# Rotation tables of an S5 scan as a background task of their own, in a one-core decoder block

## The chip, the core and the metric

The kernel runs on one core of a Trainium2 chip. The time is device microseconds of one launch; lower is better. The kernel's own comparison is a median of three runs.

## The reference

One decoder layer on 256 tokens of width 2048, in float32. Three branches read the same normalised input, are gated, summed and projected, and a squared-ReLU MLP follows.

```python
xn = rms_norm(x, norm_mix_g)
u_s5, u_lru, q, k, v, gate_logits = split(xn @ w_in)          # 2048 -> 5*1024 + 3*2048
g_s5, g_lru, g_attn = split(sigmoid(gate_logits + b_gate))    # three gates, 2048 wide each

# S5: 64 groups of 16 channels and 64 complex states, a diagonal linear recurrence over time
h = linear_scan(lam_bar, b_bar * u_s5)                        # h[t] = lam_bar*h[t-1] + ...
y = gelu(Re(C h) + d * u_s5);  y_s5 = y * sigmoid(y @ w_glu + b_glu)
# RG-LRU: causal convolution, two block-diagonal gates, a real linear recurrence
y_lru = rglru_branch(u_lru)
# stick-breaking attention, 8 heads of 128: exp(log_sigmoid(z) + sums of log_sigmoid(-z)) weights
y_attn = stick_breaking_attention(q, k, v)

h = x + (g_s5*(y_s5 @ w_br_s5) + g_lru*(y_lru @ w_br_lru) + g_attn*(y_attn @ w_br_attn)) @ w_out
out = rms_norm(h + relu(rms_norm(h) @ w_up)**2 @ w_down)
```

## The kernel before, in words

All weights stream through the core once, in **units** of 256 rows by 512 columns (512 KB). The text numbers them from 0 in the order of the list `stream`. For each unit a DMA from SyncE's queue brings `raw`; ScalarE rounds it to `hi` (the CAST of L146); VectorE forms `lo = raw - hi` (L147); TensorE then multiplies with the activations, which are split into hi and lo in the same way: hi·hi, lo·hi and hi·lo, three matmuls of 512 columns. In `chunk_tok` (lines 241 to 243) a unit has 12 such matmuls, in `chunk` (225 to 227) it has 24 of 256 columns. `raw`, `hi` and `lo` have three buffers each, so the CAST of unit i waits until TensorE is done with unit i-3, and the load of unit i until `lo` of unit i-3 is made.

A chunk is all units of 512 output columns. Order of the units: 0 to 31 the inputs of LRU and S5; 32 to 79 four times a gate chunk (8 units) and a branch chunk of the LRU (4 units); 80 to 127 keys, queries and values of two groups of four heads; 128 to 175 four times a gate chunk and a branch chunk of attention; 176 to 191 two gate chunks of S5; 192 to 199 its `w_glu`; then its branch chunks, `w_out` and the MLP. A gate chunk ends with two VectorE operations that add the bias (`gates`, L750) and two Sigmoids on ScalarE (L751); a branch chunk ends with two or four VectorE operations that multiply by the gate and add to `merged` (L760, or L762 and L763).

Everything else runs beside this stream, as generators. `later(gens, rate)` puts a task on the list `side`; after each unit `pump()` gives every task `rate` steps; `finish(task)` takes all the steps that are left. So the source order is: unit, some steps of each task, unit. The tile framework then orders each engine's instructions with a scheduler of its own, within the data dependences, and each engine executes its list strictly in that order; hence a listing of the built program is needed to know what stands behind what.

The S5 scan (`s5_scan`, a task with 1.27 steps per unit) works in 8 blocks b. The complex recurrence is made real by rotating with cosine and sine tables of the phase at each step: `s5_tables(b)` makes the tables `tc` and `ts` of 128x1024 each. Its instructions: a sum of two phase parts on VectorE (L604), rounding to whole turns on ScalarE (an Identity with a large bias, L606) and on VectorE (L607), an Abs on ScalarE (L609) and two Sin on ScalarE (L610, L611). A block needs: four small matmuls `ps_v` and their copies to `s_v` (L652), six multiplications and sums of 128x1024 with the block's own tables (L660 to L670), eight scans (L705), six more such operations (L681 to L692), a matmul `ps_y` and one VectorE operation into `us5` (L700). While a block runs, the tables of the next are made, by `next(more, None)` at three places of the code: the sum of L604 after L670, L606 and L607 after the scans, Abs and both Sin after L683. `s5_split` and `s5_stack` prepare the next block's inputs (VectorE and ScalarE operations into `ux`, twelve DMAs of 64 KB into `stk`).

`gelu` (a Square and a Tanh on ScalarE, two VectorE operations) runs after every second block, as a task. `attention` computes per head a chain of Abs, Exp and Ln on ScalarE (L796 to L798), sums along the keys on TensorE, and one more Exp (L811).

ScalarE holds one set of function tables at a time. Where two functions of different sets follow each other in its list, an ACT_TABLE_LOAD stands between them. Sin is in another set than Sigmoid and Tanh, and Exp and Ln in a third.

Of the kernel before, what the change touches and what calls it, by code (L numbers as in the profile page):

```python
# [46 lines left out]
def hybrid_block(ctx: ExitStack, tc: tile.TileContext, io, out):  # L47
# [61 lines left out]
    raw, hi, anchor = {}, {}, {}  # L109
    st = {"load": 0, "split": 0, "use": 0}  # L110

# [120 lines left out]
    def chunk_tok(name, c, k, xs, hold=0, done=None):  # L232
        ng = k // (P * UK)
# [11 lines left out]
        for g in range(ng - hold):  # L245
            (nm, cc, _), wh, wl = next_unit()
            assert (nm, cc) == (name, c)
            for kk in range(UK):
                for j in range(len(cols)):
                    mm = mms(j, g * UK + kk, wh[:, kk, :], wl[:, kk, :])  # L250
            anchor["pe"] = mm.ins
            pump()
        held = [next_unit() for _ in range(hold)]
# [339 lines left out]
    S5_RATE = 1.27  # L593

    def s5_tables(b):
# [7 lines left out]
        def gen():  # L603
            nc.vector.tensor_tensor(c, fhi[:, q, :].unsqueeze(3).broadcast_to(sh), flo[:, q, :].unsqueeze(2).broadcast_to(sh), ALU.add)  # L604
            yield
            nc.scalar.activation(sf, cf, AF.Identity, bias=magic)  # L606
            nc.vector.scalar_tensor_tensor(sf, sf, -MAGIC, cf, ALU.add, ALU.subtract)  # L607
            yield
            nc.scalar.activation(cf, sf, AF.Abs)  # L609
            nc.scalar.activation(sf, sf, AF.Sin, scale=-TURN)  # L610
            nc.scalar.activation(cf, cf, AF.Sin, scale=-TURN, bias=half_pi)  # L611
            yield
# [18 lines left out]
    def s5_scan():  # L631
# [3 lines left out]
        tabs, more = s5_tables(0)  # L635
        yield from more
        s5_split(0)
        yield
# [4 lines left out]
        tt = nc.vector.tensor_tensor  # L643
        for b in range(WT):
            c, s = tabs
            t3 = pp.tile([P, NT, L], F32, tag="t3", name=f"t3_{b}")
            for t in range(NT):
# [5 lines left out]
                if t % 2:  # L653
                    yield
            more = iter(())
            if b + 1 < WT:
                s5_split(b + 1)
                tabs, more = s5_tables(b + 1)
                yield
            tt(t1, vr, c, ALU.mult)  # L660
# [9 lines left out]
            tt(t3, t3, vr, ALU.subtract)  # L670
            next(more, None)
            yield
            for x_ in (t1, t3):
                for t in range(NT):
# [4 lines left out]
                    yield  # L679
            next(more, None)  # L680
            tt(t2, t1, c, ALU.mult)  # L681
            yield
            tt(vr, t3, s, ALU.mult)  # L683
            next(more, None)
            yield
# [15 lines left out]
            if b % 2:  # L701
                gq.append(later([gelu(b)], 1.0))

    def tt_scan(o, r, i):
        nc.vector.tensor_tensor_scan(o, r, i, 0.0, ALU.mult, ALU.add)  # L705

    def gelu(b):
        y = us5[:, b - 1:b + 1, :]
        g1 = tmp.tile([P, 2, L], F32, tag="gate", name=f"g1_{b}", bufs=3)
        nc.scalar.activation(g1, y, AF.Square)  # L710
        nc.vector.scalar_tensor_tensor(g1, g1, 1.0 / GELU_K, y, ALU.add, ALU.mult)
        yield
        nc.scalar.activation(g1, g1, AF.Tanh, scale=GELU_C * GELU_K)
        nc.vector.scalar_tensor_tensor(y, g1, 1.0, y, ALU.add, ALU.mult)
        yield
# [19 lines left out]
    def gates(idx, c, alloc):  # L735
# [8 lines left out]

        later([bias()], 1.0)
        banks = chunk_tok("w_in", GATE0 + 4 * idx + c, D, xs)
        gts = []
        for j in range(2):
# [36 lines left out]
    def attention(hs, kT, qT, vt):  # L785
# [26 lines left out]

        tc.keep_in_program_order(nc.scalar.preload_act_table_set("natural_log_exp_and_others"))
        yield
        for i in range(7):
            if i >= 3:
                weights(hs[i - 3])
            if i < 4:
                logits(hs[i])
            yield  # L820
        while vt[0] is None:
            yield
# [348 lines left out]
```

## Time and profile before

| | |
|---|---|
| three runs | 1511.58, 1511.49, 1508.52 us; median 1511.49 us |
| the profiled execution | 1512.1 us, its span 1510.3 us |
| busy: TensorE, weight loads, VectorE, ScalarE, GpSimd | 1488.4, 1260.5, 1175.2, 782.3, 35.3 us |
| mean granted clock of TensorE | 0.995 |
| ACT_TABLE_LOADs | 33, of 1283 ns each |

In the profile an instruction is named by its line of the kernel, its engine, and `out<-in` with the tiles' names. A matmul row shows about 0.39 us, but the next one starts 0.227 us later, since matmuls overlap; a wait of TensorE is best read from the starts. The profile names what ended a wait behind an arrow. Times are microseconds from the start of the span.

### The profile page before, as it was taken

What the parts mean: (1) busy time and instruction counts of PE and PEld (TensorE: products, weight loads), DVE (VectorE), ACT (ScalarE), POOL (GpSimd) and SP (SyncE); (2) the same over time, 40 slices, a digit from 0 to 9 for tenths busy, and PEclk for the clock granted to TensorE, in tenths of its full rate; (3) what the DMA queues carried; (4) which work ended last, traced back from release to release, by engine and by line L of the source; (5) the groups of instructions that cost most, each with busy time, mean ns of one, the idle gap of its engine ahead of it and who ended that gap; (6) DMA issues with size and microseconds to landing.
All of it is one profiled execution on the core that took longest, in us unless ns stands there. A gap on an engine that the chain in (4) does not pass through costs nothing.

```text
span 1510.3 us, 19900 instructions
## 1 busy us (share of the span) xinstructions
PE 1488.4 (99%) x7518; PEld 1260.5 (83%) x7518; DVE 1175.2 (78%) x1468; ACT 782.3 (52%) x920; POOL 35.3 (2%) x60
## 2 busy tenths in 40 slices
PE   9999999999999999999999999999999999999997
PEld 9997788989887878988887888888888888888886
DVE  6767998897988989689799796568854787558965
ACT  6767556565765564544455544344433444344443
POOL 1400000000000000000000000000000000000011
PEclk9999999999999999999999999999999999999999
DMA  9546766665555666666855666666666666666664
GB/s 287 157 153 176 228 205 201 187 182 168 175 172 183 208 182 210 189 202 190 276 182 188 197 184 205 194 185 196 198 194 193 193 195 195 195 191 191 192 197 152
DMA packets 89858, 292.41 MB, mean 194 GB/s; under 512 B 12834, under 2 KB 17058, under 8 KB 89634
## 3 DMA queue, kind: packets, MB, share of 16 engines
q1 hardware_dynamic: 89618, 291.07, 62.6%
q8 instruction: 59, 0.97, 0.3%
q14 instruction: 37, 0.30, 0.1%
q10 hardware_dynamic: 144, 0.07, 0.0%
HBM read 282.71 MB, written 2.10 MB: 189 GB/s over the span
## 4 chain that ended last, share of the span: by engine, by line
PE 83%; DVE 9%; issue 3%; ACT 2%; DMA 2%; SPq 0%; DVEq 0%; ACTq 0%
PE mt_w_up L242 6%; PE mt_w_up L241 6%; PE mt_w_up L243 6%; PE mt_w_in L242 5%; PE mt_w_in L243 5%; PE mt_w_in L241 5%; PE mt_w_down L242 4%; PE mt_w_down L241 4%; PE mt_w_down L243 4%; PE mp_w_down L277 4%; PE mp_w_down L278 4%; PE mp_w_down L276 4%; PE mm_w_in L227 4%; PE mm_w_in L225 4%; PE mm_w_in L226 4%; DVE lo L147 3%
## 5 line engine op out<-in xcount | busy, mean ns | idle before, releaser
L146 ACT CAST hi<-raw 128x1024 fp32r<-128x1024 f32 (+1 forms) x521 | 545.2, 1049 | 625.9 <-PE mt_w_up L243 131.4
L147 DVE TENSOR_TENSOR lo<-raw,hi 128x1024 fp32r<-128x1024 f32 (+1 forms) x521 | 637.9, 1225 | 287.7 <-ACT hi L146 284.1
L242 PE MATMUL mt_w_in<-lo,xhi 128*128 128x512 f32 x448 | 176.1, 393 | 3.9 <-DVE lo L147 3.7
L241 PE MATMUL mt_w_in<-hi,xhi 128*128 128x512 f32 x448 | 175.2, 396 | 0.2 <-ACT hi L146 0.2
L243 PE MATMUL mt_w_in<-hi,xlo 128*128 128x512 f32 x448 | 175.2, 391 | 0.0
L241 PE MATMUL mt_w_up<-hi,hhi 128*128 128x512 f32 x448 | 174.3, 389 | 0.0
L242 PE MATMUL mt_w_up<-lo,hhi 128*128 128x512 f32 x448 | 174.3, 389 | 0.0
L243 PE MATMUL mt_w_up<-hi,hlo 128*128 128x512 f32 x448 | 174.3, 389 | 0.0
L227 PE MATMUL mm_w_in<-xhi,lo 128*128 128x256 f32 x512 | 145.4, 286 | 4.5 <-DVE lo L147 4.5
L225 PE MATMUL mm_w_in<-xhi,hi 128*128 128x256 f32 x512 | 146.5, 286 | 0.5 <-ACT hi L146 0.4
L226 PE MATMUL mm_w_in<-xlo,hi 128*128 128x256 f32 x512 | 145.7, 285 | 0.0
L728 DVE STREAM_TRANSPOSE reluT<-relu 32x256 f32<-32x256 f32 x256 | 111.5, 436 | 4.2
L242 PEld LDWEIGHTS mt_w_in<-lo,xhi 128*128 128x128 f32 x448 | 84.6, 189 | 24.0 <-DVE lo L147 7.6
L227 PEld LDWEIGHTS mm_w_in<-xhi,lo 128*128 128x128 f32 x512 | 98.7, 194 | 5.5 <-DVE lo L147 5.5
L242 PE MATMUL mt_w_down<-lo,hd_hi 128*128 128x512 f32 (+1 forms) x272 | 102.5, 377 | 0.0
L241 PE MATMUL mt_w_down<-hi,hd_hi 128*128 128x512 f32 (+1 forms) x272 | 102.4, 377 | 0.0
L243 PE MATMUL mt_w_down<-hi,hd_lo 128*128 128x512 f32 (+1 forms) x272 | 102.4, 376 | 0.0
L225 PEld LDWEIGHTS mm_w_in<-xhi,hi 128*128 128x128 f32 x512 | 99.2, 194 | 1.1 <-ACT hi L146 1.0
L277 PE MATMUL mp_w_down<-lo,hd_hi 128*128 128x512 f32 x256 | 99.8, 390 | 0.1
L278 PE MATMUL mp_w_down<-hi,hd_lo 128*128 128x512 f32 x256 | 99.6, 389 | 0.0
L276 PE MATMUL mp_w_down<-hi,hd_hi 128*128 128x512 f32 x256 | 99.6, 389 | 0.0
L241 PEld LDWEIGHTS mt_w_in<-hi,xhi 128*128 128x128 f32 x448 | 84.5, 189 | 17.8 <-ACT hi L146 0.7
(299 smaller groups left out, 2370.2 us busy)
## 6 DMA issues: line engine op xcount, KB each, us to landing
raw<-in_w_in SPq DMA_DIRECT2D x175, 512.0 KB, 4.3
raw<-in_w_up SPq DMA_DIRECT2D x128, 512.0 KB, 4.2
raw<-in_w_down SPq DMA_DIRECT2D x128, 512.0 KB, 4.2
raw<-in_w_out SPq DMA_DIRECT2D x32, 512.0 KB, 4.2
raw<-in_w_br_lru SPq DMA_DIRECT2D x16, 512.0 KB, 4.6
raw<-in_w_br_attn SPq DMA_DIRECT2D x16, 512.0 KB, 4.1
raw<-in_w_br_s SPq DMA_DIRECT2D x16, 512.0 KB, 4.1
stk<-ux SPq DMA_DIRECT2D x96, 64.0 KB, 4.1
```

Source lines behind the costliest of these rows:

```text
L146: anchor["act"] = nc.scalar.copy(h[:, k, :], r[:, k, :]).ins
L147: anchor["dve"] = nc.vector.tensor_tensor(l_[:, k, :], r[:, k, :], h[:, k, :].bitcast(F32), ALU.subtract).ins
L225: nc.tensor.matmul(o, wh[:, kk, s], xh, start=first and ct % 2 == 0, stop=False, skip_group_check=True)
L226: nc.tensor.matmul(o, wh[:, kk, s], xl, start=False, stop=False, skip_group_check=True)
L227: mm = nc.tensor.matmul(o, wl[:, kk, s], xh, start=False, stop=last and ct % 2 == 1, skip_group_check=True)
L241: nc.tensor.matmul(banks[j], xh[:, s], wh[:, a:b], start=kt == 0, stop=False)
L242: nc.tensor.matmul(banks[j], xh[:, s], wl[:, a:b], start=False, stop=False)
L243: return nc.tensor.matmul(banks[j], xl[:, s], wh[:, a:b], start=False, stop=kt == ng * UK - 1)
L276: nc.tensor.matmul(o, xh[:, s], wh[:, kk, :], start=kt == 0, stop=False)
L277: nc.tensor.matmul(o, xh[:, s], wl[:, kk, :], start=False, stop=False)
L278: mm = nc.tensor.matmul(o, xl[:, s], wh[:, kk, :], start=False, stop=kt == ng * UK - 1)
L728: nc.vector.transpose(d_[32 * a:32 * a + 32, :, :, 32 * b:32 * b + 32], s_[32 * b:32 * b + 32, :, :, 32 * a:32 * a + 32])
```

## The change

The steps of the next block's tables are taken out of `s5_scan` and become a task of their own (`later([chain_of(3, more)], S5_RATE)`): it waits three steps and then runs at 1.27 steps per unit. Two empty steps are put in, and a loop that waits with the Sin while the attention task is in its chains (`st["chain"]`), or while a gate chunk is being multiplied with fewer than three units left (`st["gate"]`, `st["left"]`). GELU's Tanh waits while attention is in its chains. At the head of a block `finish(more)` takes what is left of the tables. The number of instructions is the same on every engine, the 33 table loads included.

```diff
@@ chunk_tok
             anchor["pe"] = mm.ins
+            st["left"] = ng - 1 - g
             pump()
@@ s5_tables
         def gen():
             nc.vector.tensor_tensor(c, fhi[...], flo[...], ALU.add)
             yield
+            yield
             nc.scalar.activation(sf, cf, AF.Identity, bias=magic)
             nc.vector.scalar_tensor_tensor(sf, sf, -MAGIC, cf, ALU.add, ALU.subtract)
             yield
+            yield
             nc.scalar.activation(cf, sf, AF.Abs)
+            yield
+            while st["chain"] or st["gate"] and st["left"] < 3:
+                yield
             nc.scalar.activation(sf, sf, AF.Sin, scale=-TURN)
             nc.scalar.activation(cf, cf, AF.Sin, scale=-TURN, bias=half_pi)
             yield
@@ s5_scan
         tabs, more = s5_tables(0)
         yield from more
+        more = None
...
         for b in range(WT):
+            if more is not None:
+                finish(more)
             c, s = tabs
...
-            more = iter(())
             if b + 1 < WT:
                 s5_split(b + 1)
                 tabs, more = s5_tables(b + 1)
+                more = later([chain_of(3, more)], S5_RATE)
                 yield
...
-            next(more, None)          # at three places of the block
+    def chain_of(n, gen):
+        for _ in range(n):
+            yield
+        yield from gen
@@ gelu
         yield
+        while st["chain"]:
+            yield
         nc.scalar.activation(g1, g1, AF.Tanh, scale=GELU_C * GELU_K)
@@ gates
         later([bias()], 1.0)
+        st["gate"] = True
         banks = chunk_tok("w_in", GATE0 + 4 * idx + c, D, xs)
+        st["gate"] = False
@@ attention
         tc.keep_in_program_order(nc.scalar.preload_act_table_set("natural_log_exp_and_others"))
+        st["chain"] = True
         yield
         for i in range(7):
             ...
+        st["chain"] = False
```

Since the first tables now take more steps too, the whole scan stands two to four units later in the lists than before. Three places show what the scheduler makes of it. From `pump` in `chunk_tok` on, the lines of the changed kernel have numbers that are 1 to 17 higher (the CAST stays L146 and `lo` L147): L616 and L617 are the two Sin, L605 and L609 the VectorE steps of the tables, L766 the Sigmoid, L669 to L679 the first six long operations of a block, L716 its scans, L775 and L777/L778 the ends of the branch chunks.

ScalarE's list at the end of the second gate chunk of attention (units 140 to 147), from the CAST of unit 150 to that of unit 151. Before:

```order
L146 CAST hi_4654<-raw_4623 128x1024
L609 ACTIVATE tc_4380<-ts_4381 128x1024
L610 ACT_TABLE_LOAD
L610 ACTIVATE ts_4381<-ts_4381 128x1024
L751 ACT_TABLE_LOAD
L751 ACTIVATE gate_1_0_4644<-gate_1_0_4644 128x512
L751 ACTIVATE gate_1_1_4647<-gate_1_1_4647 128x512
L611 ACT_TABLE_LOAD
L611 ACTIVATE tc_4380<-tc_4380,half_pi 128x1024
L146 CAST hi_4676<-raw_4652 128x1024
```

After:

```order
L146 CAST hi_4652<-raw_4623 128x1024
L616 ACT_TABLE_LOAD
L616 ACTIVATE ts_4443<-ts_4443 128x1024
L766 ACT_TABLE_LOAD
L766 ACTIVATE gate_1_0_4642<-gate_1_0_4642 128x512
L766 ACTIVATE gate_1_1_4645<-gate_1_1_4645 128x512
L617 ACT_TABLE_LOAD
L617 ACTIVATE tc_4442<-tc_4442,half_pi 128x1024
L146 CAST hi_4673<-raw_4650 128x1024
```

The Abs has left this place; both Sin and the three loads around the Sigmoids have stayed.

VectorE's list in the third gate chunk of the LRU and after it, from `lo` of unit 67 to `lo` of unit 70. Before:

```order
L147 TENSOR_TENSOR lo_2184<-raw_2162,hi_2183 128x1024
L670 TENSOR_TENSOR t_1_2034<-t_1_2034,s_v 128x1024
L604 TENSOR_TENSOR tc_2094<-fhi,flo 128x1024
L705 SCALAR_TENSOR_TENSOR s_t<-rad,s_t 128x256
L147 TENSOR_TENSOR lo_2208<-raw_2181,hi_2207 128x1024
L705 SCALAR_TENSOR_TENSOR s_t<-rad,s_t 128x256
L147 TENSOR_TENSOR lo_2230<-raw_2205,hi_2229 128x1024
L705 SCALAR_TENSOR_TENSOR s_t<-rad,s_t 128x256
L760 TENSOR_TENSOR merged<-mt_w_br_lru_0_64_2160,gate_2_0_2154 128x512
L760 TENSOR_TENSOR merged<-mt_w_br_lru_1_64_2161,gate_2_1_2157 128x512
L147 TENSOR_TENSOR lo_2257<-raw_2227,hi_2256 128x1024
```

After:

```order
L147 TENSOR_TENSOR lo_2181<-raw_2159,hi_2180 128x1024
L673 TENSOR_TENSOR s_t<-s_t 128x1024
L675 TENSOR_TENSOR t_1_2089<-s_v,tc_1695 128x1024
L147 TENSOR_TENSOR lo_2201<-raw_2178,hi_2200 128x1024
L677 TENSOR_TENSOR s_v<-s_v,ts_1696 128x1024
L605 TENSOR_TENSOR tc_2130<-fhi,flo 128x1024
L147 TENSOR_TENSOR lo_2221<-raw_2198,hi_2220 128x1024
L679 TENSOR_TENSOR t_1_2089<-t_1_2089,s_v 128x1024
L609 SCALAR_TENSOR_TENSOR ts_2131<-ts_2131,tc_2130 128x1024
L775 TENSOR_TENSOR merged<-mt_w_br_lru_0_64_2157,gate_2_0_2151 128x512
L775 TENSOR_TENSOR merged<-mt_w_br_lru_1_64_2158,gate_2_1_2154 128x512
L147 TENSOR_TENSOR lo_2247<-raw_2218,hi_2246 128x1024
```

The scan's long operations stand later, so that three of them and both VectorE steps of the next tables (L605, L609) now stand among these four `lo`, in place of three scans (`s_t`).

VectorE's list about the third gate chunk's end of attention, up to `lo` of unit 166. Before, from `lo` of unit 163:

```order
L147 TENSOR_TENSOR lo_4964<-raw_4939,hi_4963 128x1024
L705 SCALAR_TENSOR_TENSOR s_t<-rad,s_t 128x256 x2
L147 TENSOR_TENSOR lo_4990<-raw_4961,hi_4989 128x1024
L705 SCALAR_TENSOR_TENSOR s_t<-rad,s_t 128x256
L762 TENSOR_TENSOR gate_2_0_4931<-mt_w_br_attn_0_160_4937,gate_2_0_4931 128x512
L147 TENSOR_TENSOR lo_5012<-raw_4987,hi_5011 128x1024
L705 SCALAR_TENSOR_TENSOR t_6_4785<-rad,t_6_4785 128x256
L763 TENSOR_TENSOR merged<-merged,gate_2_0_4931 128x512
L762 TENSOR_TENSOR gate_2_1_4934<-mt_w_br_attn_1_160_4938,gate_2_1_4934 128x512
L147 TENSOR_TENSOR lo_5038<-raw_5009,hi_5037 128x1024
```

After, from L605 behind `lo` of unit 163 (L675 stands ahead of that `lo`, L677 behind it):

```order
L605 TENSOR_TENSOR tc_4884<-fhi,flo 128x1024
L679 TENSOR_TENSOR t_6_4821<-t_6_4821,s_v 128x1024
L147 TENSOR_TENSOR lo_4978<-raw_4954,hi_4977 128x1024
L716 SCALAR_TENSOR_TENSOR s_t<-rad,s_t 128x256
L609 SCALAR_TENSOR_TENSOR ts_4885<-ts_4885,tc_4884 128x1024
L147 TENSOR_TENSOR lo_5002<-raw_4975,hi_5001 128x1024
L716 SCALAR_TENSOR_TENSOR s_t<-rad,s_t 128x256
L777 TENSOR_TENSOR gate_2_0_4927<-mt_w_br_attn_0_160_4933,gate_2_0_4927 128x512
L777 TENSOR_TENSOR gate_2_1_4930<-mt_w_br_attn_1_160_4934,gate_2_1_4930 128x512
L778 TENSOR_TENSOR merged<-merged,gate_2_0_4927 128x512
L778 TENSOR_TENSOR merged<-merged,gate_2_1_4930 128x512
L147 TENSOR_TENSOR lo_5031<-raw_4999,hi_5030 128x1024
```

Here too long operations and both table steps have moved in among the `lo`, and the four operations at the end of the branch chunk, spread over three units before, now stand in one piece.

More of the change, by code (lines that the diff above doesn't have):

```diff
@@ L109, in hybrid_block @@
     raw, hi, anchor = {}, {}, {}
-    st = {"load": 0, "split": 0, "use": 0}
+    st = {"load": 0, "split": 0, "use": 0, "gate": False, "left": 0, "chain": False}
     def pieces(i):
@@ L679, in s5_scan @@
                     yield
-            next(more, None)
             tt(t2, t1, c, ALU.mult)
@@ L683, in s5_scan @@
             tt(vr, t3, s, ALU.mult)
-            next(more, None)
             yield
```

## The prediction

> **What bounds the kernel now.** I read the page, then the busy times by stretch, then TensorE's waits in the stretch that the change touches, then the rows about each wait.
>
> ```profile
> span 1510.3 us, 19900 instructions
> PE 1488.4 (99%) x7518; PEld 1260.5 (83%) x7518; DVE 1175.2 (78%) x1468; ACT 782.3 (52%) x920; POOL 35.3 (2%) x60
> ```
>
> TensorE is the bound. The change adds and takes away no matmul, so it can pay only where TensorE waits, and cost only where it makes TensorE wait.
>
> ```profile
> core 0: us, PE busy (x) PEld busy (x) DVE busy (x) ACT busy (x) POOL busy (x), PEclk, DMA share, GB/s
> 113.00:210.00 97.00, 93.43 (x420) 74.63 (x420) 80.69 (x92) 60.25 (x74) 0.00 (x0) 0.98 0.67 199
> 210.00:455.00 245.00, 245.00 (x1531) 217.64 (x1530) 212.89 (x249) 151.22 (x195) 0.00 (x0) 1.00 0.61 184
> 455.00:475.00 20.00, 19.61 (x86) 15.67 (x86) 18.65 (x22) 8.60 (x10) 0.00 (x0) 1.00 0.69 207
> 475.00:495.00 20.00, 17.63 (x75) 13.50 (x77) 15.32 (x17) 13.32 (x14) 0.00 (x0) 0.91 0.44 143
> 495.00:610.00 115.00, 114.93 (x566) 94.17 (x559) 103.94 (x114) 64.70 (x76) 0.00 (x0) 1.00 0.67 204
> ```
>
> The scan's tables are made from 113 to 610 us. TensorE is idle there for 3.57 + 0.39 + 2.37 + 0.07 = 6.4 us, and at the head of two stretches the clock was halved: 0.91 over 20 us means (1 - 0.91) x 20 / 0.5 = 3.6 us at half speed. VectorE is busy for 77% to 93% of these stretches (15.32 of 20, 18.65 of 20 us): it has little left.
>
> ```profile
> PE mt_w_in L242 <- DVE lo L147: 3.7, 5, 1.9
> PE mt_w_br_attn L241 <- ACT hi L146: 2.2, 1, 2.2
> ```
>
> One long wait is ScalarE's (`hi`, behind the sines), five are VectorE's (`lo`). The change is aimed at the first kind. Its new loops wait while the program is written, not on the chip: what they do there is the order alone.
>
> **Step 1, unit 151 (the end of a gate chunk): -2.5 us.** The rows before:
>
> ```profile
> 473.81 1.06 ACT L146 CAST hi<-raw 128x1024 fp32r<-128x1024 f32 x1 [0.49 <-PE mt_w_in L243]
> 474.77 1.05 ACT L609 ACTIVATE tc<-ts 128x1024 f32<-128x1024 f32 x1
> 475.84 1.28 ACT L610 ACT_TABLE_LOAD   x1
> 477.13 1.06 ACT L610 ACTIVATE ts<-ts 128x1024 f32<-128x1024 f32 x1
> 478.20 1.28 ACT L751 ACT_TABLE_LOAD   x1
> 479.50 1.15 ACT L751 ACTIVATE gate<-gate 128x512 f32<-128x512 f32 x2
> 480.65 1.28 ACT L611 ACT_TABLE_LOAD   x1
> 481.95 1.15 ACT L611 ACTIVATE tc<-tc,half_pi 128x1024 f32<-128x1024 f32 x1
> 483.00 2.92 ACT L146 CAST hi<-raw 128x1024 fp32r<-128x1024 f32 x3
> ...
> 481.31 0.39 PE L242 MATMUL mt_w_br_attn<-lo,ya_hi 128*128 128x512 f32 x1
> 481.54 0.39 PE L243 MATMUL mt_w_br_attn<-hi,ya_lo 128*128 128x512 f32 x1
> 484.08 0.73 PE L241 MATMUL mt_w_br_attn<-hi,ya_hi 128*128 128x512 f32 x2 [2.15 <-ACT hi L146]
> 486.06 0.63 PE L242 MATMUL mt_w_br_attn<-lo,ya_hi 128*128 128x512 f32 x1
> 486.48 0.63 PE L243 MATMUL mt_w_br_attn<-hi,ya_lo 128*128 128x512 f32 x1
> ```
>
> The next matmul was due at 481.54 + 0.23 = 481.77 and came at 484.08: 2.31 us. Behind it matmuls start 0.42 us apart (486.06, 486.48), not 0.23: that is the half clock, and 3.6 us of it lose 3.6 x (1 - 0.227/0.42) = 1.65 us. The listing of the changed kernel still has Sin, Sigmoid and Sin with three loads ahead of the CAST of unit 151; only the Abs is gone. So: CAST to 474.87, load to 476.15, Sin to 477.21, load to 478.50, Sigmoids to 479.65, load to 480.93, Sin to 482.08, CAST, which starts 0.1 before that ends, to 483.05. TensorE waits 1.33 us, 0.98 less. A wait that short I expect to leave the clock alone, for the two that halved it lasted 2.06 us (below) and 2.31 us; then 1.65 us go too. Together -2.6, taken as -2.5. Ends: -1.0, if the clock still halves, and -4.0, if the whole wait goes.
>
> The Trainium skill (TensorE: Matmul & The Clock Gate, Part 1, "What's actually happening") lets the clock fall back only after at least one idle window of about 3.4 us. By that rule waits of 2.06 and 2.31 us would not have halved it; the trace disagrees, and I go by the trace. By the rule this step would be worth -1.0 and the sum below would be 1.5 us higher.
>
> **Step 2, units 36 to 57 (the first tables, LRU's end): 0 us.** The rows before:
>
> ```profile
> 125.28 1.20 DVE L607 SCALAR_TENSOR_TENSOR ts<-ts,tc 128x1024 f32<-128x1024 f32 x1
> 127.30 0.69 DVE L573 TENSOR_TENSOR ylru_lo<-lru_xc,ylru_hi 128x512 fp32r<-128x512 f32 x1 [0.81 <-ACT ylru_hi L572]
> 127.90 1.22 DVE L147 TENSOR_TENSOR lo<-raw,hi 128x1024 fp32r<-128x1024 f32 x1
> 129.04 1.26 DVE L570 TENSOR_TENSOR_SCAN lru_tc<-lru_tc,lru_ts 128x256 f32<-128x256 f32 x2
> 130.22 1.20 DVE L147 TENSOR_TENSOR lo<-raw,hi 128x1024 fp32r<-128x1024 f32 x1
> ...
> 126.66 0.61 PE L241 MATMUL mt_w_in<-hi,xhi 128*128 128x512 f32 x2
> 129.18 0.50 PE L242 MATMUL mt_w_in<-lo,xhi 128*128 128x512 f32 x1 [1.91 <-DVE lo L147]
> ```
>
> Long VectorE rows start 1.14 us apart, scans and halves 0.60. TensorE wanted `lo` of unit 36 at 126.66 + 2 x 0.23 = 127.12 and got it at 129.18, 2.06 us late. In the changed list `lo` of unit 36 stands ahead of L609 (L607 of before) and takes its place at 125.28: this wait goes. But before `lo` of unit 37 there stand now a `ylru_lo`, two scans, L609 and the other `ylru_lo`. The first cannot start before 127.30, since it waits for ScalarE; then 127.30 + 0.60 + 1.18 + 1.14 + 0.60 = 130.82, and `lo` ends at 132.04. TensorE, not held up, is through unit 36 at 126.66 + 12 x 0.227 = 129.38 and wants that `lo` at 129.83: a wait of 2.2 us, one unit later, as long as the old one and as likely to halve the clock. Behind it the loads, which follow `lo`, even things out. At unit 55 both Sigmoids, a load and both Sin now stand in one piece between two CASTs, 1.15 + 1.28 + 1.06 + 1.15 = 4.6 us, where two units of TensorE give 2 x 2.72 = 5.4: some tenths of a wait, which the small waits of this stretch that go (of the 3.7 us above) pay. Ends: -3.7, if the 2.06 and its half clock go without a successor; +2.5, if unit 55 waits 1.5 us and the rest stays.
>
> **Step 3, unit 70 (VectorE): +1.0 us.** Rows before: the `lo` of unit 67, the row behind it, the group of the copies of `s_v`, and TensorE's first use of `lo` of unit 70.
>
> ```profile
> 216.46 1.23 DVE L147 TENSOR_TENSOR lo<-raw,hi 128x1024 fp32r<-128x1024 f32 x1
> 217.61 1.22 DVE L670 TENSOR_TENSOR t<-t,s_v 128x1024 f32<-128x1024 f32 x1
> ...
> L652 ACT COPY s_v<-ps_v 128x512 f32<-128x512 f32 x32 | 17.2, 587 | 3.4 <-PE ps_v L650 3.2
> ...
> 228.32 0.39 PE L242 MATMUL mt_w_in<-lo,xhi 128*128 128x512 f32 x1
> ```
>
> By the listing there stand behind this `lo` now six long operations, three `lo` and two halves: 217.61 + 9 x 1.14 + 2 x 0.60 = 229.07. TensorE wants the last of them at 228.32: 0.7 us late, and a unit whose `lo` is late starts with two matmuls on `hi`, which gives 0.2 back. Unit 67's `lo` itself will be later than 217.69, by up to 0.9 us: four copies of `s_v`, 4 x 0.59 us, stand between the CASTs of units 64 and 65 where two stood (1.2 us more, of which some is slack). So 0.5 to 1.5; I take 1.0. The other end is 0, if VectorE gets ahead before.
>
> **Step 4, units 163 to 172: +1.8 us.**
>
> ```profile
> 516.93 1.21 DVE L147 TENSOR_TENSOR lo<-raw,hi 128x1024 fp32r<-128x1024 f32 x1
> ...
> 524.09 0.39 PE L242 MATMUL mt_w_in<-lo,xhi 128*128 128x512 f32 x1
> 529.53 0.39 PE L242 MATMUL mt_w_in<-lo,xhi 128*128 128x512 f32 x1
> ...
> 540.18 0.39 PE L241 MATMUL mt_w_in<-hi,xhi 128*128 128x512 f32 x1
> 540.64 0.50 PE L242 MATMUL mt_w_in<-lo,xhi 128*128 128x512 f32 x1
> ```
>
> The first row is `lo` of unit 162, the matmuls are the first uses of `lo` of units 164, 166 and 170. Behind `lo` of unit 162 there now come L675, `lo`, L677, L605, L679 and `lo` of unit 164: 518.07 + 6 x 1.14 = 524.91, 0.8 us after 524.09. Then a scan, L609, `lo`, a scan, four halves, `lo` of unit 166: 6 x 0.60 + 3 x 1.14 = 7.0, at 531.9; TensorE, 0.9 later than before, wants it at 529.53 + 0.9 + 0.2 = 530.6: another 1.3. With 0.1 lost at each restart, 2.4 us. In return the sines, which stood at units 169 to 171 with their Abs, come where there is room, and the wait at 540.64 (540.18 to 540.64, 0.23 too many) goes with two like it: -0.6. Ends: -0.6 and +3.0.
>
> **Step 5, the rest: +0.5 us.** In units 142 to 147 `lo` of unit 143 becomes punctual and that of unit 146 late, by the same shift; at most the 0.39 us of idle of 455 to 475 can go. The end of the scan stands two units later, and the last values for `w_glu` come as they are wanted. 0 to 1.2 for both. The twelve `stk` DMAs of a block move with the scan on SyncE's queue, past two or three loads of weights each time; they share the loads' bandwidth as before, and I set that at nothing, since DMAs are at 0.44 to 0.69 here. Tables and GELU in the middle (210 to 455 us, no idle) are hidden by TensorE's slow chunks and by attention's extra matmuls, and I count nothing; if that cover is short, the `lo` behind L609 in the key chunk (unit 90) is late next.
>
> **Sum:** -2.5 + 0 + 1.0 + 1.8 + 0.5 = +0.8 us, so a span of 1511.1 and, with the 1.8 us outside it, 1512.9 us. The profiled execution (1512.1) lies 0.6 above the median of the three runs, so **1512.3 us** for a median.
>
> A measurement of this kernel tells 0.2%, 3.0 us, from no change.
>
> **Rivals.**
> *VectorE's piles halve the clock (slower).* The waits of units 55, 70 and 166 are each set at 1 to 1.5 us. At about 2 us within one stretch the clock halves, as in units 36 and 151, at 1.65 us each. Two of them: 0.8 + 3.3 = +4.1, 1515.6 us. For it: VectorE's 93% in 455 to 475 and 90% in 495 to 610, and the packed lists. Against it: before, VectorE's waits at the same density were short but for one.
> *The sines stay where they hurt (slower).* The listing shows three loads in a row at unit 151. If a late `gate` operand takes back the Abs's 1.05 us, the wait stays 2.3 us and the clock halves: +0.8 + 2.5 = +3.3, 1514.8 us.
> *VectorE gets ahead (faster).* While the scan is late it does nothing for VectorE; if that lets `lo` run up to its limit of three buffers, steps 3 and 4 give 0 and -0.6, and the sum is -2.5 + 0 + 0 - 0.6 + 0.5 = -2.6, with a wait less at units 36 and 37 (-2.0) -4.6: 1506.9 us. For it: 210 to 455 has no idle at all. Against it: 9 x 1.14 us is more than the 8.2 us that TensorE needs for three units.
>
> **How the numbers follow.** My forecast, a near tie, 0.53; the piles 0.20, the sines 0.10; VectorE ahead 0.17. The last three lie about or beyond 3.0 us. So faster 0.17, same 0.53, slower 0.30. The range takes the faster rival's end, 1506.5, and the slower one's with a further wait of 1.9 us, 1517.5.
>
> **What would show it.** Right: at unit 151 three loads and a wait of 1.0 to 1.6 us with PEclk 1.00 behind; a wait for `lo` of about 2 us at unit 37 in place of 36; waits for `lo` at units 70, 164 and 166 of 0.5 to 1.5 us. Wrong: no waits there, or half-clock rows behind them.

## Result and profile after

The changed kernel takes 1514.08 us (median of 13 runs, 1512.60 to 1515.15); the kernel before, in runs taken between them, 1511.21 us (13 runs, 1508.52 to 1513.38). The ratio is 1.0019, with a 95% interval of 1.0011 to 1.0027: some 2.9 us slower, where +0.8 was forecast. The profiled execution took 1514.19 us, that of before 1512.1.

The busy times of the five stretches after:

```profile
113.00:210.00 97.00, 93.51 (x416) 75.17 (x417) 78.97 (x90) 59.81 (x72) 0.00 (x0) 0.98 0.67 202
210.00:455.00 245.00, 244.54 (x1531) 217.50 (x1529) 212.96 (x249) 151.40 (x194) 0.00 (x0) 1.00 0.60 184
455.00:475.00 20.00, 19.48 (x86) 15.67 (x85) 19.73 (x23) 9.78 (x10) 0.00 (x0) 1.00 0.66 200
475.00:495.00 20.00, 17.00 (x67) 13.08 (x66) 13.86 (x17) 12.90 (x13) 0.00 (x0) 0.91 0.47 142
495.00:610.00 115.00, 114.07 (x557) 92.05 (x556) 104.97 (x114) 63.40 (x73) 0.00 (x0) 1.00 0.65 202
```

The work is the same and the waits are more: TensorE is idle for 8.4 us from 113 to 610, 6.4 before, and the stretch from 475 to 495 still runs at a mean clock of 0.91. Its waits in that part, by what ended them:

```profile
PE mt_w_in L242 <- DVE lo L147: 5.6, 7, 2.4
PE mt_w_br_attn L241 <- ACT hi L146: 2.4, 1, 2.4
```

The wait that the change was aimed at (`mt_w_br_attn`) has not become shorter, and VectorE's have grown from 3.7 to 5.6 us. Unit by unit, by the start of each unit's first matmul: at unit 34 the execution after is 1.23 us ahead of the one before (a difference from the start of the program, where nothing was changed), at unit 205 it is 1.12 us behind. The 2.35 us between are lost and won so (each row runs from the start of its first unit to the start of the unit behind its last, and both kernels have the same number of matmuls in it):

| units | forecast | measured |
|---|---|---|
| 36 to 62 | 0 | -0.5 |
| 70 | +1.0 | +0.8 |
| 71 to 141 | 0 | -0.6 |
| 142 to 149 | in step 5 | +0.1 |
| 150 to 152 | -2.5 | -0.3 |
| 153 to 157 | nothing named | +1.2 |
| 158 to 176 | +1.8 | +1.1 |
| 190 to 195 | in step 5 | +0.5 |

Unit 151, ScalarE's timeline, then TensorE's:

```profile
470.84 1.05 ACT L146 CAST hi<-raw 128x1024 fp32r<-128x1024 f32 x1 [2.50 <-DMA raw<-in_w_br_attn]
473.63 1.05 ACT L146 CAST hi<-raw 128x1024 fp32r<-128x1024 f32 x1 [1.74 <-DMA raw<-in_w_br_attn]
474.70 1.28 ACT L616 ACT_TABLE_LOAD   x1
476.00 1.06 ACT L616 ACTIVATE ts<-ts 128x1024 f32<-128x1024 f32 x1
477.06 1.28 ACT L766 ACT_TABLE_LOAD   x1
478.36 1.15 ACT L766 ACTIVATE gate<-gate 128x512 f32<-128x512 f32 x2
479.51 1.28 ACT L617 ACT_TABLE_LOAD   x1
480.81 1.15 ACT L617 ACTIVATE tc<-tc,half_pi 128x1024 f32<-128x1024 f32 x1
481.86 2.92 ACT L146 CAST hi<-raw 128x1024 fp32r<-128x1024 f32 x3
...
482.94 1.22 PE L241 MATMUL mt_w_br_attn<-hi,ya_hi 128*128 128x512 f32 x2 [2.40 <-ACT hi L146]
...
484.91 0.63 PE L242 MATMUL mt_w_br_attn<-lo,ya_hi 128*128 128x512 f32 x1
485.34 0.63 PE L243 MATMUL mt_w_br_attn<-hi,ya_lo 128*128 128x512 f32 x1
```

The burst of three loads, two Sin and two Sigmoids is there, without the Abs, 7.2 us between two CASTs. But the CAST ahead of it (unit 150, at 473.63) is now late itself: it had to wait for its weights (`<-DMA raw`). Before, that CAST came as soon as TensorE had freed its buffer (`<-PE`). TensorE waited 2.57 us (2.31 before), and the clock was halved again (0.43 us from 484.91 to 485.34). From CAST to CAST the burst is 1.0 us shorter than before (8.23 us, 9.20 before), but against the start of TensorE's unit 149 its first CAST stands 1.2 us later; so the wait has grown by 0.26 us. That units 150 to 152 together still take 0.3 us less comes from behind the wait, where TensorE lost 0.5 us less; why is open.

VectorE ahead of `lo` of unit 146 (465.81), whose end lets the load of unit 149 go:

```profile
460.69 1.22 DVE L605 TENSOR_TENSOR tc<-fhi,flo 128x1024 f32<-128x1024 f32 x1
461.82 1.22 DVE L147 TENSOR_TENSOR lo<-raw,hi 128x1024 fp32r<-128x1024 f32 x1
462.96 1.22 DVE L679 TENSOR_TENSOR t<-t,s_v 128x1024 f32<-128x1024 f32 x1
464.10 0.69 DVE L716 TENSOR_TENSOR_SCAN s_t<-rad,s_t 128x256 f32<-128x256 f32 x1
464.69 1.21 DVE L609 SCALAR_TENSOR_TENSOR ts<-ts,tc 128x1024 f32<-128x1024 f32 x1
465.81 1.23 DVE L147 TENSOR_TENSOR lo<-raw,hi 128x1024 fp32r<-128x1024 f32 x1
```

No row shows idle time: VectorE is full, and both table steps (L605, L609) stand ahead of that `lo`. The matmuls that waited for a `lo`, in TensorE's timeline, at units 37, 70, 146, 154 and 166:

```profile
131.16 0.79 PE L242 MATMUL mt_w_in<-lo,xhi 128*128 128x512 f32 x1 [2.39 <-DVE lo L147]
...
227.46 0.50 PE L242 MATMUL mt_w_in<-lo,xhi 128*128 128x512 f32 x1 [0.46 <-DVE lo L147]
...
467.09 0.50 PE L242 MATMUL mt_w_in<-lo,xhi 128*128 128x512 f32 x1 [0.52 <-DVE lo L147]
...
494.00 0.50 PE L242 MATMUL mt_w_in<-lo,xhi 128*128 128x512 f32 x1 [0.59 <-DVE lo L147]
...
530.86 0.50 PE L242 MATMUL mt_w_in<-lo,xhi 128*128 128x512 f32 x1 [0.84 <-DVE lo L147]
```

All but the fourth were named in the prediction.

### The profile page after: what moved, and what is told of

Same layout as the page of the kernel before. It is cut to its first block, busy times and chain, and to the rows that moved or that the text cites. A ratio compares the mean times of both kernels' runs of the same rounds, so it can differ in the third digit from the quotient of the medians.

```text
span 1511.9 us, 19898 instructions
## 1 busy us (share of the span) xinstructions
PE 1486.8 (98%) x7518; PEld 1258.4 (83%) x7518; DVE 1176.8 (78%) x1468; ACT 783.0 (52%) x920; POOL 36.0 (2%) x60
## 4 chain that ended last, share of the span: by engine, by line
PE 81%; DVE 10%; ACT 3%; issue 3%; DMA 2%; SPq 0%; DVEq 0%; ACTq 0%
PE mt_w_up L242 6%; PE mt_w_up L241 6%; PE mt_w_up L243 6%; PE mt_w_in L242 5%; PE mt_w_in L243 5%; PE mt_w_in L241 5%; PE mt_w_down L242 4%; PE mt_w_down L241 4%; PE mt_w_down L243 4%; DVE lo L147 4%; PE mp_w_down L278 4%; PE mp_w_down L279 4%; PE mp_w_down L277 4%; PE mm_w_in L227 3%; PE mm_w_in L225 3%; PE mm_w_in L226 3%
## 5 line engine op out<-in xcount | busy, mean ns | idle before, releaser
L146 ACT CAST hi<-raw 128x1024 fp32r<-128x1024 f32 (+1 forms) x521 | 545.8, 1050 | 629.3 <-PE mt_w_up L243 130.6
L147 DVE TENSOR_TENSOR lo<-raw,hi 128x1024 fp32r<-128x1024 f32 (+1 forms) x521 | 638.1, 1226 | 283.3 <-ACT hi L146 279.4
```

Of the source, the lines that this page charges most:

```text
L146: anchor["act"] = nc.scalar.copy(h[:, k, :], r[:, k, :]).ins
L147: anchor["dve"] = nc.vector.tensor_tensor(l_[:, k, :], r[:, k, :], h[:, k, :].bitcast(F32), ALU.subtract).ins
```

## Experiments

Theory A: the change loses at unit 151 what it was to win, because the sines stay between the Sigmoids and the early table steps delay a load; and the same steps make `lo` late at units 70, 146 and 164 to 166. Against it stand B (TensorE would wait at unit 151 anyway, for something else) and C (all `lo` are late since the scan stands two units later, whatever the tables do). Times are medians; the ratio is to the kernel before in the same runs, with its interval.

**1. One table step made short.** Does the late load explain the burst's late start?

```diff
-nc.vector.scalar_tensor_tensor(sf, sf, -MAGIC, cf, ...)
+w_ = 64 if b == 6 else 1024
+nc.vector.scalar_tensor_tensor(sf[:, 0:w_], sf[:, 0:w_], -MAGIC, cf[:, 0:w_], ...)
...                              # both Sin of block 6 get another scale
```

> The changed kernel, but for the tables of block 6 alone the second table step on VectorE (L609) works on 64 of its 1024 columns; the rest of those tables is left unrounded and the two Sin take a smaller scale, so their values mean nothing. The lists of all engines keep their order; only this one instruction, which stands ahead of `lo` of unit 146, is about 1.0 us shorter. Theory A (the Abs's 1.05 us was taken back by loads): `lo` of unit 146 is on time, so the wait of 0.8 us at 467 goes; the load of unit 149, issued behind that `lo`, comes about 1 us earlier, so do the CASTs of units 149 and 150 and the whole burst behind them, and TensorE's wait at unit 151 falls from 2.6 to 1.4 to 1.7 us. If the clock then stays full: 0.8 + 1.0 + 1.65 = 3.4 us less than the changed kernel, 1510.7 us; if it still halves, 1.8 less, 1512.3. Rival B (the operands of the Sigmoids, or the place of the burst itself, set the wait): the wait at unit 151 stays at 2.3 us or more and only the 0.8 goes, 1513.3 us.

1511.87 us, 1.0007 (0.9998 to 1.0016), 2.2 us below the changed kernel. ScalarE's and TensorE's timelines:

```profile
470.74 1.05 ACT L146 CAST hi<-raw 128x1024 fp32r<-128x1024 f32 x1 [1.49 <-DMA raw<-in_w_br_attn]
473.50 1.05 ACT L146 CAST hi<-raw 128x1024 fp32r<-128x1024 f32 x1 [1.70 <-DMA raw<-in_w_br_attn]
...
482.81 0.73 PE L241 MATMUL mt_w_br_attn<-hi,ya_hi 128*128 128x512 f32 x2 [1.96 <-ACT hi L146]
```

TensorE starts unit 146 at 467.01 here and at 465.96 in the changed kernel. Counted from there, the CASTs of units 149 and 150 come 1.15 and 1.18 us earlier, and 0.74 us of the wait at unit 146 are gone. So the one step did hold the loads back, and through them the burst. What the expectation forgot: TensorE, not held up at 146, is itself 0.74 us earlier at unit 151. Its wait there fell only from 2.57 to 2.12 us, and the clock was still halved. Together 1.2 us. By the starts of the units, 0.8 of that comes in units 142 to 149 and 0.55 in units 153 to 157; units 150 to 152 gain nothing (12.53 us, 12.41 in the changed kernel), since the shorter wait was lost again behind it. The median is 0.4 below the time expected with a half clock. The trace has a further 1.3 us in units 36 to 62, which this edit does not touch: no half clock followed the wait at unit 37 this time.

**2. No loop, and 10. half the loop.**

```diff
-while st["chain"] or st["gate"] and st["left"] < 3:     # run 2: no loop at all
-    yield
+while st["chain"]:                                      # run 10: this half alone
+    yield
```

> The changed kernel without the loop that holds the two Sin back. In the lists the Sin of block 6 then stand in one piece between the CASTs of units 148 and 149, and the Sigmoids between those of 149 and 150, with two loads less; at unit 129 they stand singly among attention's last exponentials, with two loads more. Theory A (the loop itself keeps the sines at the end of the gate chunk): the wait at unit 151 and its half clock go, 2.6 + 1.65 = 4.2 us; at unit 129 ScalarE has 4 x 1.28 + 1.06 + 1.15 us and three exponentials and the two copies of v between two CASTs, about 9.5 us where TensorE's next three units give 8.2, which costs 1 to 3.5 us (the latter with a half clock); at unit 53 and 54 nothing changes by more than some tenths. Sum -3.2 to -0.7, 1510.9 to 1513.4 us. Rival B (TensorE waits there for something else, loads of weights): -1 or less at unit 151, and the sum is at or above the changed kernel, 1514 to 1517.

> The changed kernel with the half of the loop alone that holds the Sin back during attention's chains; the half for gate chunks is left out. In the lists the Sin of block 6 stand in one piece behind the CAST of unit 148 and the Sigmoids behind that of 149, as without any loop, while attention's exponentials at unit 129 stay undisturbed; at unit 53 the two Sin stand ahead of the two Sigmoids with two loads, 7.1 us with the CAST's between two CASTs. Theory A (the half for gate chunks costs, the half for chains pays): 4.2 us less at unit 151, 1.5 to 3.5 us more at unit 55 (the latter with a half clock): 1511.4 to 1513.4 us, and 2.3 to 4.4 us less than the run without any loop. Rival B: the wait at unit 151 comes back a unit later; 1514 us or more.

Without the loop 1515.76 us, 1.003 (1.0019 to 1.0042); with the half for chains alone 1509.57 us, 0.9991 (0.9981 to 1.0000), 4.5 below the changed kernel. In both, unit 151 waits for nothing: what B says of that unit falls. But the time without the loop lies in B's range and above A's, because the loss at units 129 to 141 was larger than A had it, and units 53 to 57 lost too, where A saw next to nothing. ScalarE in attention's chain without the loop, and the matmul behind it (unit 130):

```profile
413.03 1.28 ACT L614 ACT_TABLE_LOAD   x1
...
419.68 1.28 ACT L824 ACT_TABLE_LOAD   x1
...
423.64 0.79 PE L241 MATMUL mt_w_in<-hi,xhi 128*128 128x512 f32 x1 [3.49 <-ACT hi L146]
```

Four loads lie between these times, two for each Sin among the Exp. TensorE waits 3.65 us, and two windows of half clock follow (422.22 to 429.04 us): units 129 to 141 take 46.77 us, 40.23 in the changed kernel and in run 10. The half for chains is worth these 6.5 us; the medians of the two runs differ by 6.2. The half for gate chunks costs: it puts off the Sin, which would run in one piece behind the CAST of unit 148, until the gate chunk is over, and so right onto its Sigmoids. Leaving it out has a price of its own at unit 54, a wait of 1.94 us for `hi` and two windows of half clock in the profile of run 10 (1.24 us and one window without the loop); that run still came out 1.8 us below its expected range, in part because the waits at units 164 to 166 shrank too (from 1.35 to 0.54 us).

**3. The sines held out of the branch chunk's start.**

```diff
-while st["chain"] or st["gate"] and st["left"] < 3:
+while st["chain"] or st["gate"] and st["left"] < 3 or st["branch"] and st["left"] > 1:
...                              # st["branch"] is set while a branch chunk is multiplied
```

> The changed kernel with one condition more: the Sin also wait while a branch chunk has more than one unit left. In ScalarE's list the two Sin then stand in one piece, with one load, between the CASTs of units 152 and 153; between 150 and 151 there are only the two Sigmoids. Theory A: the whole wait at unit 151 goes with its half clock, 2.6 + 1.65 = 4.2 us, less a wait of up to 0.8 at unit 153 (load and two Sin, 3.5 us, where TensorE has three units); nothing else moves. 1509.9 to 1510.7 us, which is 0.5 to 1.3 below the kernel before. Rival B (a late load or `lo` shows at the same place): 1.5 or less gained, 1512.6 or more.

1506.68 us, 0.9969 (0.9958 to 0.9981): 7.4 us below the changed kernel, more than A had. ScalarE from the CAST of unit 150, and the stretch:

```profile
471.89 1.05 ACT L146 CAST hi<-raw 128x1024 fp32r<-128x1024 f32 x1 [1.71 <-DMA raw<-in_w_br_attn]
472.85 1.16 ACT L766 ACTIVATE gate<-gate 128x512 f32<-128x512 f32 x2
473.91 1.04 ACT L146 CAST hi<-raw 128x1024 fp32r<-128x1024 f32 x1
...
475.00:495.00 20.00, 20.00 (x102) 16.01 (x101) 19.15 (x21) 11.54 (x12) 0.00 (x0) 1.00 0.63 198
```

The CAST of unit 151 now follows 2.0 us behind that of 150, not 8.2, and the stretch has neither idle time nor half clock. In units 150 to 152 TensorE gains 4.2 us on the changed kernel, as expected: that is what the burst cost.

Another 1.2 us come in units 153 to 157, where the changed kernel waits for `lo` of unit 154. One would take that wait for an echo of the burst, since VectorE stood idle for 6.14 us in front of `lo` of unit 151 and had its list behind it. But run 10 has no burst, and the wait is there all the same. VectorE, and TensorE's matmul behind it, in run 10; then VectorE in run 3:

```profile
489.89 1.28 DVE L777 TENSOR_TENSOR gate<-mt_w_br_attn,gate 128x512 f32<-128x512 f32 x2
491.09 1.28 DVE L778 TENSOR_TENSOR merged<-merged,gate 128x512 f32<-128x512 f32 x2
492.29 1.22 DVE L147 TENSOR_TENSOR lo<-raw,hi 128x1024 fp32r<-128x1024 f32 x1
...
493.56 0.51 PE L242 MATMUL mt_w_in<-lo,xhi 128*128 128x512 f32 x1 [0.66 <-DVE lo L147]
```

```profile
484.73 0.68 DVE L779 TENSOR_TENSOR gate<-mt_w_br_attn,gate 128x512 f32<-128x512 f32 x1
485.33 1.22 DVE L147 TENSOR_TENSOR lo<-raw,hi 128x1024 fp32r<-128x1024 f32 x1
486.46 0.69 DVE L780 TENSOR_TENSOR merged<-merged,gate 128x512 f32<-128x512 f32 x1
```

In run 10, as in the changed kernel, the four operations at the end of the branch chunk stand in one piece ahead of that `lo`; in run 3 the `lo` of units 153 and 154 stand among them, and the last comes behind both. Units 153 to 157 take 15.81 us before and in run 3, 17.02 in the changed kernel, and 16.81 in runs 2 and 10. So by this comparison at most 0.2 of the 1.2 us can be an echo (run 6 shows where the rest comes from). The other 2 us of the profiled executions are a half clock behind unit 37 that this one did not have, and a shorter wait there, 2.06 us for 2.55 (see the end).

**4. Only the sines of one block moved, in the kernel before.**

```diff
 nc.scalar.activation(cf, sf, AF.Abs)
+if b == 6:
+    yield
 ...
 tt(t1, t1, vi, ALU.add)
+next(more, None)
```

> The kernel before, in which only the two Sin of block 6's tables are taken one step of the code later, so that they stand in one piece between the CASTs of units 153 and 154; the Abs stays between 150 and 151, and one Sigmoid stands on either side of the CAST of unit 151. Nothing of the task, the pauses or the loops is in it. Theory A (the burst at unit 151 was worth its wait and its half clock, and the rest of the change costs what it gains): 2.31 + 1.65 = 4.0 us gained, 1507.2 us. Rival B (something else is late at unit 151 next): 1.5 or less gained, 1509.7 or more.

1506.93 us, 0.9971 (0.9961 to 0.9982), 4.5 us gained where 4.0 were expected. Step 1's other end was right, and nothing of the task is needed for it.

**5. The scan at its old place, tables as a task; 6. the scan late, tables as before.**

```diff
# run 5, on the changed kernel: the first tables without pauses and loop
-yield
+if b:
+    yield
# run 6, on the kernel before
 yield from more
+yield
+yield
+yield
```

Run 5 has the second pause, the step behind the Abs and the loop only for `b` above 0 as well. In runs 5 and 9 the loop is also lifted while `finish(more)` takes the last steps.

> The changed kernel, but the first tables are made without the new pauses and without the loop, so that the scan stands where it stood before the change; the tables of blocks 1 to 7 remain a task of their own, with their VectorE steps (L605, and L609, here L610) early, among the six long operations and the first scans. In the lists the two Sin of block 6 stand behind the CAST of unit 145, away from the gate chunk's end; at unit 54 they stand on both sides of the Sigmoids, with three loads. Theory A (the waits for `lo` come from the early table steps, wherever the scan stands): 4.0 us gained at unit 151 against the kernel before, waits for `lo` of 2 to 4 us in all at units 67 to 70, 142 to 146 and 160 to 166, and 0.5 to 2 us at unit 55 for the three loads: 1509.5 to 1513.5 us. Rival C (the waits come from the scan standing two units later): those waits together under 1 us more than before, and 1507.9 to 1510 us.

> The kernel before with three empty steps behind the first tables and nothing else: the whole scan stands two to three units later, its tables as before (three places of the code, Abs and both Sin together). The lists then have the Sin of block 6 behind the CAST of unit 153 in one piece, only by the shift, and the Sigmoids alone at 150. Theory A: 4.0 us gained at unit 151, and no new wait for `lo` above 0.5 us at units 70, 146, 154 and 164 to 166, where the changed kernel has 0.6 to 1.0: 1507.2 us, within 1. Rival C (the late scan makes these waits): they are there as in the changed kernel, 2.5 to 3.5 us in all, 1509.7 to 1510.7 us.

Run 5: 1512.22 us, 1.0007 (0.9998 to 1.0016). Run 6: 1511.72 us, 1.0000 (0.9991 to 1.0009). Both gain 4 us or more at unit 151 in their traces. Run 5 gives it back by early table steps though its scan is not late: `lo` waits for instance at unit 142,

```profile
460.68 0.50 PE L242 MATMUL mt_w_in<-lo,xhi 128*128 128x512 f32 x1 [1.02 <-DVE lo L147]
```

and by the three loads at unit 55 (1.68 us for `hi`). At unit 49 it has 1.09 us of the same kind. At units 70, 146 and 160 to 166, however, it has no wait over 0.3 us, though its expectation had 2 to 4 us in all for such places, unit 142 among them. Run 6 has none over 0.3 us at units 70, 146 and 164 to 166 either. So the late scan alone does not make these waits, and C falls for these places; but the early steps alone do not make them there: it takes both. At unit 154 run 6 has 0.64 us, and units 153 to 157 take 16.91 us: this wait is C's, the shift alone makes it, and it costs 1.1 us. (Before, twenty small matmuls of the scan stood in unit 153 and gave VectorE 1.7 us; with the late scan they come behind it. Run 3 has the late scan too and does not wait there, with the operations of the branch chunk spread.)

But run 6 was not 4 us faster: the shift put the Abs and both Sin of the next tables ahead of the Sigmoids of the last LRU gate chunk (unit 77), and TensorE waited for `hi` for 1.37 us, then for `lo` for 0.69, and ran at half clock behind it, 3.3 us in all:

```profile
250.00 0.74 PE L241 MATMUL mt_w_br_lru<-hi,ylru_hi 128*128 128x512 f32 x2 [1.21 <-ACT hi L146]
...
252.26:255.67 3.41, 3.41 (x9) 2.63 (x8) 3.41 (x5) 0.58 (x1) 0.00 (x0) 0.50 0.47 155
```

My expectation had looked at unit 151 alone and missed the same thing in an earlier chunk.

**7. and 8. The first tables' L609 behind unit 37.**

```diff
# run 7, on the kernel before; run 8 moves run 3's pauses to the same place
+for _ in range(0 if b else 3):
+    yield
 nc.scalar.activation(sf, cf, AF.Identity, bias=magic)
```

> As the run with three empty steps, but these stand ahead of the rounding of the first tables (L606 and L607), so that besides the shift of the scan the VectorE step L607 of the first tables moves from ahead of `lo` of unit 36 to behind that of unit 37; nothing of the task or the loops is in it. Theory A (that step is what TensorE waits for at unit 36): the wait of 2.07 us at unit 36 falls to under 1.0 and no window of half clock follows it, 1.1 to 3.7 us less than with the three steps alone: 1503.5 to 1506.1 us. Rival B (LRU's last scans and ScalarE's ylru_hi set that wait): it only moves to unit 37, as in the changed kernel, and the time is that of the three steps alone, 1507 us or more.

> The changed kernel with the Sin held out of the first units of branch chunks (as in the third run), and the pauses of the first tables put ahead of their rounding: the scan stands as in the changed kernel, but L609 of the first tables stands behind `lo` of unit 37, not ahead of it. Theory A: the wait at unit 37 (2.06 to 2.55 us in the changed kernel's and the third run's profiles) falls by 1.1 us or more and never halves the clock: 1.1 to 2.8 us less than the third run, 1503.9 to 1505.6 us. Rival B (ylru_hi of ScalarE sets that wait): within 0.5 of the third run, 1506.2 to 1507.2 us.

Run 7: 1510.47 us, 0.9998 (0.9989 to 1.0006). Run 8: 1508.02 us, 0.9978 (0.9969 to 0.9987), 1.3 above run 3. Both lie above A's ranges; run 7 lies in B's, run 8 above B's too. Run 7 is 1.25 us below run 6, its like with the three steps alone, which is within the difference that A named, but in units 36 to 62 the two traces differ by 0.4 us only. The wait at unit 37 did fall, to 0.83 and 0.40 us. But the displaced steps came back a few units later; run 7's TensorE:

```profile
130.06 0.50 PE L242 MATMUL mt_w_in<-lo,xhi 128*128 128x512 f32 x1 [0.67 <-DVE lo L147]
139.45 0.50 PE L242 MATMUL mt_w_br_lru<-lo,ylru_hi 128*128 128x512 f32 x1 [0.51 <-DVE lo L147]
...
```

With two more at units 43 and 44, and with their restarts left out, these are 0.83 + 0.68 + 0.90 + 0.70 = 3.1 us, where one wait of 2.07 us (and its half clock) stood. Run 8 lost most at another place: its units 153 to 157 take 17.28 us, 1.5 more than run 3's; the CAST of unit 153 had to wait 1.47 us for its weights there, and what made them late is open.

**9. Three blocks' table steps among the scans.** On run 3:

```diff
-more = later([chain_of(3, more)], S5_RATE)
+more = later([chain_of(10 if b in (1, 5, 6) else 3, more)], S5_RATE)
```

> The third run (Sin held out of the first units of branch chunks), in which the tables made in blocks 1, 5 and 6 start 10 instead of 3 steps after their task is set up. Their VectorE steps L605 and L609 then stand among the last scans (units 73 and 75, 149 and 151, 168 and 170) and not among the six long operations; the scan itself stands as in the changed kernel, and the Sin stay in one piece, away from Sigmoids. Theory A (these two steps make the waits of `lo` at units 70, 146 and 164 to 166): the waits at these places, 0.72 + 0.83 + 0.36 + 1.2 = 3.1 us in the third run's profile, go, with at most 0.5 us of new ones: 2.6 to 3.1 us less than the third run, 1503.6 to 1504.1 us. Rival B (VectorE has no room anywhere in these stretches, so a step that is moved makes another `lo` late): the waits come back behind the new places, and the time is within 1 us of the third run, 1506 to 1507.5 us.

1505.45 us, 0.9963 (0.9950 to 0.9975): the lowest median here, 5.35 us under the kernel before in the same runs and 8.6 under the changed kernel's median. It lies between A's range and B's, and the intervals of runs 3 and 9 overlap, so the times do not show run 9 to be the faster. Two of its stretches:

```profile
475.00:495.00 20.00, 20.00 (x101) 15.70 (x100) 19.54 (x21) 12.66 (x13) 0.00 (x0) 1.00 0.59 195
495.00:610.00 115.00, 115.00 (x586) 95.99 (x585) 103.63 (x113) 66.14 (x80) 0.00 (x0) 1.00 0.64 203
```

No idle time and no half clock is left from 475 to 610 us, and against run 3 the trace gains 3.3 us from unit 58 on, a little more than A expected: moved to where the short scans leave room, the steps make no other `lo` late. So the trace bears A out at these places. The medians lie only 1.2 us apart. In the profiled execution a half clock behind unit 37 (2.23 us of wait there) takes 1.7 of the 3.3 back; what the other executions lost was not seen.

The change's other part, GELU's loop, was not run alone: with it alone the built program has the lists of the kernel before on every engine.

## Why the prediction was right in its time and wrong in a step

The time lay in the range, and the direction and most terms held. The forecast of +0.8 us was 2.1 too low, and one step accounts for most of that.

- **Step 1 failed (-2.5, measured -0.3).** It priced the lists from the old time of the CAST of unit 150, 474.87, as if only the Abs were gone. That CAST was bound by TensorE before; after, it is bound by a load, which waits for a `lo` that the same change made late (run 1: 1.15 us from one table step). The step looked at ScalarE's list from that CAST on, and not at what releases the CAST. With -0.3 in its place the sum is +3.0; the medians differ by 2.9. That they agree so well is partly luck: in the traces the other terms were 2.0 us too high in all, and units 153 to 157, which no step named, take 1.2 of that back. The rival "the sines stay where they hurt" gave 1514.8 and the right wait, 2.3 us or more, but by a late `gate` operand; it was a late load. Its chance of 0.10 was too small.
- **The Trainium skill's rule.** The wait of 2.57 us halved the clock. The Trainium skill (TensorE: Matmul & The Clock Gate, Part 1, "What's actually happening") asks for an idle window of about 3.4 us; the traces disagree, and the last section has what they show instead. "A wait of 1.33 us leaves the clock alone" was not put to the test at unit 151, for the wait never was so short. Elsewhere such waits did not always leave it alone: 1.37 us (run 6, unit 78) and 1.24 us (run 2, unit 54) for `hi`, each with 0.7 us for `lo` close behind, halved the clock; 1.68 us (run 5, unit 55) did not. The step left out the wait for `lo` that can follow.
- **Step 2 held (0, measured -0.5).** The wait moved from unit 36 to 37, with 2.55 us and a half clock; small waits before it went.
- **Step 3 held (+1.0, measured +0.8)**, at the place named.
- **Step 4 was a little high (+1.8, measured +1.1).** New waits of 0.25, 0.1 and 1.0 us at units 164 to 166, 1.7 with their restarts, where 2.4 were forecast; the 0.6 in return came as forecast.
- **Step 5 held (+0.5, measured +0.6):** unit 143 punctual, unit 146 late by 0.8, the tail 0.5. What it missed is that unit 146 feeds step 1.
- **Not in any step:** units 153 to 157, 1.2 us. The shift of the scan alone makes 1.1 of it (run 6). The prediction looked at the places where long operations moved in among the `lo`, not at one where matmuls that had covered VectorE moved out.
- **The piles** halved no clock: no wait of `lo` behind unit 37 was longer than 1.0 us. **VectorE got no further ahead**: no `lo` of steps 3 and 4 was early.

The loop did the reverse of its words at this place: it holds the sines while the gate chunk has fewer than three units left and lets them go when it is over, which is when the Sigmoids are due. A condition in the order of the code is one chunk's end too early for a list that runs three units ahead.

## What to carry to other kernels

When a burst on one engine stalls another, look at both sides of it: what it holds up, and what lets it start; a step taken out of the burst is worth nothing if its start moves back by as much. Where two functions of different tables meet, keep each set in one piece (here 4.2 us at the place itself; the one condition more that did it lowered the median by 7.4), and check every place where the condition opens, not only where it closes. On an engine without idle time a moved step makes another operand late, unless it goes among short instructions (by the traces, run 9 against runs 7 and 8). Before a second wait is called an echo of a first, look for a run that has the second without the first (run 10).

## What the runs showed of the hardware

Whether a wait of about 2 us halves TensorE's clock is set by where it falls. All twelve profiled executions have the same wait at 92 us, in a part that no kernel here changes, of 1.92 to 1.94 us in the timeline. Behind it the clock was halved in five and full in seven. The kernel before, then after: TensorE's row, and windows of 3.41 us, laid so that one of them is the halved stretch (before) or a whole number of windows away from one (after).

```profile
92.31 0.42 PE L227 MATMUL mm_w_in<-xhi,lo 128*128 128x256 f32 x1 [1.93 <-DVE lo L147]
...
89.11:92.52 3.41, 1.48 (x12) 1.27 (x11) 3.41 (x7) 1.32 (x2) 0.00 (x0) 1.00 0.20 82
92.52:95.93 3.41, 3.41 (x17) 3.41 (x17) 3.41 (x7) 0.00 (x0) 0.00 (x0) 0.50 0.73 180
```

```profile
91.88 0.38 PE L227 MATMUL mm_w_in<-xhi,lo 128*128 128x256 f32 x1 [1.93 <-DVE lo L147]
...
90.25:93.66 3.41, 1.78 (x15) 1.79 (x16) 3.41 (x6) 1.04 (x1) 0.00 (x0) 1.00 0.20 38
93.66:97.08 3.42, 3.42 (x31) 3.42 (x30) 3.26 (x7) 1.05 (x1) 0.00 (x0) 1.00 0.78 259
```

Before, the whole wait lies in one window; after, a part of it lies in the window ahead. In both kernels the halved stretches are one window long each, but for the one at the program's end, and begin a whole number of windows apart (92.52, 130.07 and 485.05 before, 11 and 104 windows). By the starts of the matmuls, with gaps of 0.15 us and more counted, every window at full clock with 1.9 us or more of idle time was followed by a half clock, and none with less than 1.8; between these it went either way (1.83 without, 1.82 and 1.84 with). So each wait of 2 to 3 us costs its length and, depending on where it falls, 1.7 us more. In runs 2 and 10 two halved windows came in a row, with 1.6 and 0.6 us of idle time in the first; what a window that is itself halved needs is not shown. The executions of one program scatter in part with this: run 10 took 1513.14 us at a mean clock of 0.995 and 1506.80 us at 0.999. But in runs 3 and 4 the slower executions did not have the lower clock, so something else is in the scatter too.
